# Five seams of a two-layer mLSTM and attention trunk: values ahead of the recurrence, later gate steps, output-projection weights and banks in other places, squares in groups

## The chip, the cores and the metric

The kernel runs on one core of one Trainium2 chip. The metric is the device time of one execution in microseconds (us); the time quoted for a kernel is the median of its runs. PE is the matmul engine (TensorE), DVE is VectorE, ACT is ScalarE, POOL is GpSimd, SP is the engine that issues most transfers. Arithmetic is float32; inputs and output lie in HBM.

## What is computed

The reference is a trunk of two layers on 1024 positions of width 1024. Cut to what matters here:

```python
def hybrid_layer(x, norm1_g, w_in, conv_w, gate_i_b, gate_f_b, head_norm_g, w_out, norm2_g, w_up, w_down):
    h = rms_norm(x, norm1_g)
    mq, mk, mv, mo, mi, mf, aq, ak, av = jnp.split(h @ w_in, ..., axis=-1)
    mq, mk = split(silu(centred_depthwise_conv(concat([mq, mk]), conv_w)))     # 5 taps
    gi = mi + gate_i_b;  gf = log_sigmoid(mf + gate_f_b)                       # per head and direction
    hm = mlstm_chunkwise(q, k, v, gi[0], gf[0]) + flip(mlstm_chunkwise(flip(q), ...))   # 4 heads of 128
    y_m = rms_norm_per_head(hm) * head_norm_g * sigmoid(mo)
    y_a = dilated_attention(rope(aq), rope(ak), av)                            # 8 heads of 64
    x = x + concat([y_m, y_a]) @ w_out
    u = relu(rms_norm(x, norm2_g) @ w_up)                                      # 1024 -> 4096
    return x + (u * u) @ w_down                                                # 4096 -> 1024

def reference(x, ...):
    for layer in range(2): x = hybrid_layer(x, ...)
    return rms_norm(x, final_g)
```

## The kernel before, in words

The activations lie transposed: 128 features on the partitions, 1024 positions along them, in two halves (tiles t = 0 and 1) of 512. Every float32 product is made of three matmuls on values split in a high and a low part: `wh`·high, `wh`·low, `wl`·high. A weight tile is fetched by SP, cast to `wh` by ACT (L80) and its remainder `wl` is made by POOL (L82). A matmul of 512 columns is the unit of most of the work.

A layer runs in this order. `norm` (L141) splits the scaled input in `hh` (ACT, L158) and `hl` (DVE, L159) and sums the squares of the eight feature tiles: `sumsq` makes a square on ACT (L106) and adds it to `acc` (L107, POOL for t = 0 and DVE for t = 1 in layer 1); there each tile's squares stand right behind its split. `gates` (L186 to 278) is a generator that computes the gate rows in three steps, each started by a `next(gates)`: the first up to the norm's `r` and the gates' projection (into PSUM tile `ps`), the second the scans on DVE and a small matmul `pa` (L253) on a row `X` (L250), the third the transposes of the gate rows to `nat` (L276, L277).

Then four mLSTM heads. `m_proj` (L281) makes four projections of a head, each 48 matmuls into two `pj` tiles (three `pj` banks in all): values (`zv`), queries and keys (`z`, then `c` by a 5-tap convolution, one ACT step L301 and four DVE steps L303), output gate (`so`). `evac_r` (L170) brings a `pj` tile to SBUF by a DVE multiply with `r` (L173). `q` and `k` are multiplied with their sigmoid at L325 (keys on DVE, queries on POOL). `m_head` (L331) builds the decay matrices `E` (a transfer, POOL L340, DVE L341), transposes `k` (PE L357), makes the chunk scores (PE L363) and runs the recurrence of eight chunks in two directions (PE L379, L381, L390; DVE L395). `m_tail` (L400) of the head before divides and sums the two directions (DVE L406 to L410, POOL L410 for the second direction, DVE L413), normalises, and transposes the result. The instructions that fill PE during a recurrence are those of the next head's projections.

Eight attention heads follow in four pairs; `a_vt` (L551) transposes a pair's values on PE (L560) and ACT copies them out (L562). During the last pair the first two of seven products of the output projection run (`out_early`, L892).

The output, up and down projections use `seven` (L820): seven products in place of eight on 2x2 blocks. `fetch` (L780) brings weight blocks `w0`, `w1`, `w2` by SP; `plus` (L787) adds another block onto one by an accumulating transfer issued by POOL (L788); `operand`, `diff` and `negsum` (L764 to L778) make the split activations (ACT cast L760, DVE L761, L770, L776). `products` (L799) issues the matmuls (L812) of one product, and `take` adds the finished banks onto the result (`add`, L818). `bank` (L790) hands out the four `ph` banks, which several products share, or in turn three `pj` and one `pi`. In the first chunk of the up projection the norm's sums of `acc` over the partitions are made on PE (`rms`, L129).

Within an engine the order of the instructions is the order of the program unless a scheduler lets a ready instruction pass: `high_priority` (L172) moves an evacuation ahead of its place, `in_order` (L724) keeps the attention as written. The pools' `order` lists (L678, L706, L734) set at which addresses tiles lie and thereby which earlier tiles must be finished before a fetch may start.

## Time and profile before

| | us |
|---|---|
| median of three runs | 2625.42 (2621.58 to 2628.07) |
| the profiled execution | 2632.46 |
| its span | 2630.7 |

| engine | busy us | share |
|---|---|---|
| PE (matmul) | 2466.7 | 94% |
| DVE | 1923.8 | 73% |
| POOL | 1405.3 | 53% |
| ACT | 1252.6 | 48% |

A busy PE is not a PE at its peak: matmuls are pipelined, so the recorded 0.39 us of one overlap those of the next, and where the clock is granted at half, the same matmul takes longer and still counts as busy. How much PE loses at a place is seen in the idle time that a view prints in brackets before an instruction, and in the granted clock of the stretch behind it.

### The profile page before, as it was taken

To read this page: it belongs to the slowest core of one execution; us is meant where nothing else is said; L and a number is where in the kernel's file an instruction comes from. 1 tells how busy PE (TensorE), PEld (TensorE's weight loads), DVE (VectorE), ACT (ScalarE), POOL (GpSimd) and SP (SyncE) were. 2 spreads that over 40 slices of the span, in tenths; PEclk is the share of its full clock that TensorE was granted. 3 is DMA by queue.
4 is the path that set the end of the run, shared out by engine and by line. 5 is a ranking of instruction groups with operands and counts; after the bars stand their busy time and mean duration, and the time that the engine had idled before them with its cause. 6 is when DMAs were issued, how large, how long until landed. Compare 5 with 4: busy or idle time off the path is not lost. (4 is left out here: it accounts for less than half of the span.)

```text
span 2630.7 us, 35982 instructions
## 1 busy us (share of the span) xinstructions
PE 2466.7 (94%) x13470; PEld 1957.5 (74%) x13470; DVE 1923.8 (73%) x2376; ACT 1252.6 (48%) x2092; POOL 1405.3 (53%) x1119
## 2 busy tenths in 40 slices
PE   7899989998999999999898999999989999999997
PEld 5778866666778888787777787666667787887876
DVE  6677666687886786867766776666788767769687
ACT  5444344464654545445444444445455445454544
POOL 4344332335677677767644343223166766767765
PEclk9999999998999999999999999999999999999999
DMA  4222100036455555555322221001365555545553
GB/s 137 89 66 69 42 25 21 27 107 152 95 111 119 102 104 111 104 112 109 90 90 78 69 66 37 25 21 58 108 128 100 105 111 105 112 104 109 113 101 84
DMA packets 119791, 231.39 MB, mean 88 GB/s; under 512 B 14768, under 2 KB 17984, under 8 KB 119616
## 3 DMA queue, kind: packets, MB, share of 16 engines
q0 software_dynamic: 46912, 93.06, 21.3%
q1 hardware_dynamic: 72704, 136.02, 16.5%
q8 instruction: 107, 1.75, 0.3%
q14 instruction: 68, 0.56, 0.1%
HBM read 220.24 MB, written 8.65 MB: 87 GB/s over the span
## 5 line engine op out<-in xcount | busy, mean ns | idle before, releaser
L82 POOL TENSOR_TENSOR wl<-w,wh 128x512 fp32r<-128x512 f32 x484 | 782.7, 1636 | 303.8 <-ACT wh L80 303.3
L812 PE MATMUL ph<-b,wh 128*128 128x512 f32 x2240 | 697.6, 393 | 15.4 <-ACT wh L80 9.8
L812 PEld LDWEIGHTS ph<-b,wh 128*128 128x128 f32 x2240 | 424.3, 190 | 106.0 <-ACT wh L80 11.7
L80 ACT CAST wh<-w 128x512 fp32r<-128x512 f32 x484 | 298.0, 618 | 428.6 <-POOL wl L82 122.7
L812 PE MATMUL ph<-b,wl 128*128 128x512 f32 x1120 | 442.5, 395 | 8.5 <-POOL wl L82 8.0
L82 POOL TENSOR_TENSOR wl<-wr,wh 128x512 fp32r<-128x512 f32 x132 | 200.2, 1519 | 451.0 <-ACT wh L80 432.7
L812 PE MATMUL pj<-b,wh 128*128 128x512 f32 x1224 | 384.0, 395 | 8.0 <-ACT wh L80 8.0
L90 PE MATMUL pj<-hh,wh 128*128 128x512 f32 x896 | 366.9, 410 | 6.4 <-DVE z L173 5.4
L92 PE MATMUL pj<-hh,wl 128*128 128x512 f32 x896 | 358.1, 400 | 0.4 <-POOL wl L82 0.4
L91 PE MATMUL pj<-hl,wh 128*128 128x512 f32 x896 | 356.4, 398 | 0.0
L761 DVE TENSOR_TENSOR b<-T,b 128x1024 fp32r<-128x1024 f32 x148 | 249.6, 1691 | 124.9 <-ACT b L760 119.7
L812 PEld LDWEIGHTS pj<-b,wh 128*128 128x128 f32 x1224 | 233.2, 191 | 59.4 <-ACT wh L80 9.3
L812 PEld LDWEIGHTS ph<-b,wl 128*128 128x128 f32 x1120 | 212.0, 189 | 64.1 <-POOL wl L82 20.6
L812 PE MATMUL pj<-b,wl 128*128 128x512 f32 x612 | 242.3, 396 | 13.5 <-POOL wl L82 13.5
L90 PEld LDWEIGHTS pj<-hh,wh 128*128 128x128 f32 x896 | 171.0, 191 | 54.7 <-issue 15.2
L92 PEld LDWEIGHTS pj<-hh,wl 128*128 128x128 f32 x896 | 170.5, 190 | 35.6 <-POOL wl L82 0.8
L91 PEld LDWEIGHTS pj<-hl,wh 128*128 128x128 f32 x896 | 171.1, 191 | 30.8 <-issue 0.5
L760 ACT CAST b<-T 128x1024 fp32r<-128x1024 f32 x148 | 155.5, 1050 | 44.5 <-DVE T L776 14.6
L788 POOL DMA_DIRECT2D w<-w_down x128 | 116.8, 945 | 74.2 <-DMA w<-w_down 38.3
L601 ACT ACTIVATE sm<-sm,nm 128x512 f32<-128x512 f32 x128 | 91.6, 717 | 131.9 <-DVE nm L599 131.9
L812 PEld LDWEIGHTS pj<-b,wl 128*128 128x128 f32 x612 | 116.6, 191 | 42.3 <-POOL wl L82 18.1
L80 ACT CAST wh<-wr 128x512 fp32r<-128x512 f32 x132 | 80.6, 614 | 139.4 <-PE pj L91 75.6
(254 smaller groups left out, 4268.0 us busy)
## 6 DMA issues: line engine op xcount, KB each, us to landing
w<-w_up SPq DMA_DIRECT2D x128, 256.0 KB, 2.7
w<-w_up POOLq DMA_DIRECT2D x128, 256.0 KB, 4.1
w<-w_down SPq DMA_DIRECT2D x128, 256.0 KB, 2.7
w<-w_down POOLq DMA_DIRECT2D x128, 256.0 KB, 4.2
wr<-w_in SPq DMA_DIRECT2D x116, 256.0 KB, 2.7
E<-gd SPq DMA_DIRECT2D x16, 512.0 KB, 4.8
qi<-gd SPq DMA_DIRECT2D x16, 512.0 KB, 5.6
w<-w_out SPq DMA_DIRECT2D x32, 256.0 KB, 5.3
```

The lines of the kernel that those rows point to most:

```text
L80: nc.scalar.copy(wh, raw)
L82: nc.gpsimd.tensor_tensor(out=wl, in0=raw, in1=wh.bitcast(F32), op=ALU.subtract)
L90: nc.tensor.matmul(ps, wh[:, j, :], xh[:, sl], start=start, stop=False)
L91: nc.tensor.matmul(ps, wh[:, j, :], xl[:, sl], start=False, stop=False)
L92: nc.tensor.matmul(ps, wl[:, j, :], xh[:, sl], start=False, stop=stop)
L601: nc.scalar.activation(sm, sm, AF.Exp, scale=-1.0, bias=nm, accum_out=l)
L760: nc.scalar.copy(hi, src)
L761: nc.vector.tensor_tensor(out=lo, in0=src, in1=hi.bitcast(F32), op=ALU.subtract)
L788: self.nc.gpsimd.dma_start(w, src, accum_op=ALU.add)
L812: nc.tensor.matmul(out, a[:, k, :], b, start=new and k + i == 0, stop=k + i == 5, skip_group_check=not new)
```

## The change

Five places are edited. (1) `m_values`, the values' projection of a head, is taken out of `m_proj` and written ahead of the `m_head` of the head before; head 0's stands ahead of the loop. (2) The second step of the gates comes behind the whole key projection (`i == 1`) and the third behind the output-gate projection. (3) In the output projection `w2` is fetched first and all eight additions onto it are issued at once, then `w1` and `w0`; the `up` pool places `sq` and `w2` ahead of `w1` and `T`; the `dn` pool places the four `ph` banks ahead of `pi`. (4) In layer 1's `norm` the squares stand in groups of four behind the splits of those four tiles. (5) The norm of the first up-projection chunk comes with the second product in place of the first, and `a_vt` copies its groups by DVE and ACT in turn.

```diff
-        for d in order:
+        for i, d in enumerate(order):
 ...
-            if L > 0:
-                squares(d)
+            if L > 0 and i % 4 == 3:
+                for x in order[i - 3:i + 1]:
+                    squares(x)
 ...
-    def m_proj(self, L, h, hs, r, mp, gates):
-
-        nc = self.nc
-        base = 1 + 4 * h
-        ps, self.ahead = self.ahead or self.proj(L, base + 3, hs), None
+    def m_values(self, L, h, hs, r, mp):
+
+        nc = self.nc
+        ps, self.ahead = self.ahead or self.proj(L, 4 + 4 * h, hs), None
         zv = mp.tile([P, S + 4], F32, name="zv", tag="z", bufs=3)
         for t in range(2):
             self.evac_r(zv[:, t * HALF:(t + 1) * HALF], ps[t], r, t)
         v1 = mp.tile([P, NC, P + 1], F32, name="v1", tag=f"v1{h % 2}", bufs=1)
         nc.gpsimd.memset(v1[:, :, P:P + 1], 1.0)
+        return zv, v1
+
+    def m_proj(self, L, h, hs, r, mp, gates, values):
+
+        nc = self.nc
+        base = 1 + 4 * h
+        zv, v1 = values
 ...
-            next(gates, None)
-            if i == 0:
+            if i == 1:
+                next(gates, None)
+            else:
 ...
             self.evac_r(so[:, t * HALF:(t + 1) * HALF], ps[t], r, t)
+        next(gates, None)
 ...
-        for lo, n, m in ((0, 4, 1), (4, 4, 1), (8, 1, 0), (9, 4, 1), (13, 4, 0)):
+        for g, (lo, n, m) in enumerate(((0, 4, 1), (4, 4, 1), (8, 1, 0), (9, 4, 1), (13, 4, 0))):
 ...
-            nc.scalar.copy(dst[:, j:j + n], pt[:, :n])
+            (nc.vector.tensor_copy if g % 2 == 0 else nc.scalar.copy)(dst[:, j:j + n], pt[:, :n])
 ...
-                pend = None
+                pend, values = None, self.m_values(L, 0, hs, r, mp)
                 for h in range(MH):
-                    prj = self.m_proj(L, h, hs, r, mp, gates)
+                    prj = self.m_proj(L, h, hs, r, mp, gates, values)
+                    if h < MH - 1:
+                        values = self.m_values(L, h + 1, hs, r, mp)
 ...
-            self.order(self.up, (("T3", S, 2), ("w1", HALF, 4), ("T", S, 2), ("w2", HALF, 4), ("w0", HALF, 4),
-                                 ("sq", HALF, SQ)))
+            self.order(self.up, (("T3", S, 2), ("sq", HALF, SQ), ("w2", HALF, 4), ("w1", HALF, 4), ("T", S, 2),
+                                 ("w0", HALF, 4)))
             with tc.tile_pool(name=f"dn{L}", bufs=1, space=PSUM, reuse_waits="tile") as self.dn:
+                self.order(self.dn, (("ph", HALF, 4), ("pi", HALF, 1)))
 ...
-        if not early:
-            w0 = self.fetch("w0", src, 0, 0)
-        w1 = self.fetch("w1", src, 0, 1)
-        w2 = self.fetch("w2", src, 1, 0)
         addto = lambda w, m, h: lambda q: self.plus(w[q], src(q, m, h))
         if early:
-            chain = P5 = None
+            w2 = self.fetch("w2", src, 1, 0)
+            for q in range(4):
+                addto(w2, 1, 1)(q)
+            for q in range(4):
+                addto(w2, 0, 0)(q)
+            w1 = self.fetch("w1", src, 0, 1)
             w0 = self.fetch("w0", src, 0, 0)
             for q in range(4):
-                addto(w2, 1, 1)(q)
-                addto(w2, 0, 0)(q)
-            for q in range(4):
                 addto(w0, 1, 0)(q)
+            chain = P5 = None
         else:
+            w0 = self.fetch("w0", src, 0, 0)
+            w1 = self.fetch("w1", src, 0, 1)
+            w2 = self.fetch("w2", src, 1, 0)
 ...
-            if n == 1 and c == 0:
+            if n == 2 and c == 0:
                 self.r2 = self.rms(acc)
```

**What moves on the engines.** The first place is PE in layer 0, head 0, where the transposes of `k` stand. Before, they follow the last matmuls of the output-gate projection (`pj_599`), with the next head's values (`pj_845`) behind them:

```order
L91 MATMUL pj_599<-hl_168,wh_632 128x512
L92 MATMUL pj_599<-hh_167,wl_634 128x512
L357 MATMUL pt_691<-ident_122,c_586 128x128 x4
L357 MATMUL pt_697<-ident_122,c_586 128x128 x4
L90 MATMUL pj_845<-hh_137,wh_849 128x512
L91 MATMUL pj_845<-hl_138,wh_849 128x512
```

After, they (now L366) follow the last matmuls of the next head's values (`pj_671`), with that head's queries (`pj_912`) and the scores (L372) behind them:

```order
L91 MATMUL pj_671<-hl_168,wh_704 128x512
L92 MATMUL pj_671<-hh_167,wl_706 128x512
L366 MATMUL pt_758<-ident_122,c_537 128x128 x4
L366 MATMUL pt_764<-ident_122,c_537 128x128 x4
L90 MATMUL pj_912<-hh_137,wh_916 128x512
L372 MATMUL pt_770<-c_452,c_537 128x128 x4
L372 MATMUL pt_777<-c_452,c_537 128x128 x4
L388 MATMUL pn_786<-v1_383,E_737 128x129
```

All 48 matmuls of the next head's values moved from behind the transposes to in front of them, and the recurrence (L388) is now filled by the next head's queries.

The second place is DVE behind the recurrence of head 0, where the queries of head 1 (`pj_912`, `pj_913`) are brought from their banks (L173, now L174). Before, the values (`zv_907`) had come out during the recurrence, and the queries stand here:

```order
L341 TENSOR_TENSOR E_1143<-nat_379,E_1143 128x1024
L413 TENSOR_TENSOR H_717<-H_717,H_718 128x8x128
L348 COPY dec_1150<-qi_1148 128x8
L417 TENSOR_REDUCE v0_1202<-H_718 128x8
L341 TENSOR_TENSOR E_1152<-nat_379,E_1152 128x1024
L173 TENSOR_TENSOR z_974<-pj_912,r_319 128x512
```

After, in the same place:

```order
L350 TENSOR_TENSOR E_1210<-nat_379,E_1210 128x1024
L357 COPY dec_1217<-qi_1215 128x8
L422 TENSOR_TENSOR H_784<-H_784,H_785 128x8x128
L174 TENSOR_TENSOR z_974<-pj_912,r_319 128x512
L350 TENSOR_TENSOR E_1219<-nat_379,E_1219 128x1024
L174 TENSOR_TENSOR z_974<-pj_913,r_319 128x512
```

The queries' evacuation moved ahead of the second `E` and stays behind the sum `H`; on PE the queries now run a projection earlier, against the recurrence.

The third place is the start of the output projection in layer 0, first on POOL. Before, the remainders of three `w1` weights stand ahead of any addition onto `w2` (the L788 transfers):

```order
L82 TENSOR_TENSOR wl_5642<-w1_5603,wh_5640 128x512
L82 TENSOR_TENSOR wl_5659<-w1_5604,wh_5657 128x512
L82 TENSOR_TENSOR wl_5676<-w1_5605,wh_5674 128x512
L788 DMA w2_5611<-w_out 128x512
L788 DMA w2_5612<-w_out 128x512
```

After:

```order
L800 DMA w2_5608<-w_out 128x512
L800 DMA w2_5605<-w_out 128x512
L82 TENSOR_TENSOR wl_5644<-w1_5621,wh_5642 128x512
L800 DMA w2_5606<-w_out 128x512
L82 TENSOR_TENSOR wl_5661<-w1_5622,wh_5659 128x512
L82 TENSOR_TENSOR wl_5678<-w1_5623,wh_5676 128x512
L800 DMA w2_5607<-w_out 128x512
L800 DMA w2_5608<-w_out 128x512
L800 DMA w0_5629<-w_out 128x512
L800 DMA w0_5630<-w_out 128x512
L82 TENSOR_TENSOR wl_5695<-w1_5624,wh_5693 128x512
```

Five additions moved ahead of the first remainder of `w1`, and four stand between its third and its fourth.

On ACT at the same place the row ahead of the first `w1` weight is, after:

```order
L772 CAST b_5719<-T_5601 128x1024
L772 CAST b_5723<-T_5602 128x1024
L80 CAST wh_5642<-w1_5621 128x512
L80 CAST wh_5659<-w1_5622 128x512
L80 CAST wh_5676<-w1_5623 128x512
L772 CAST b_5756<-T_5601 128x1024
```

Before, one of these casts of a difference `T` stands behind the first three weights:

```order
L80 CAST wh_5640<-w1_5603 128x512
L80 CAST wh_5657<-w1_5604 128x512
L80 CAST wh_5674<-w1_5605 128x512
L760 CAST b_5721<-T_5600 128x1024
L80 CAST wh_5691<-w1_5606 128x512
L760 CAST b_5754<-T_5599 128x1024
```

The second cast of `T` moved ahead of the first weight.

## Rows read from the trace of the kernel before

**Rows 1.** The page's first part: busy us, share of the span, instructions.
```profile
PE 2466.7 (94%) x13470; PEld 1957.5 (74%) x13470; DVE 1923.8 (73%) x2376; ACT 1252.6 (48%) x2092; POOL 1405.3 (53%) x1119
```

**Rows 2.** The chain of work that ended last: start us, us, engine, tile, line.
```profile
2001.09 2.72 PE pi L812 x12
```

**Rows 3.** PE's waits: what for, us in total, times, longest us.
```profile
PE pt L357 <- DVE c L325: 17.5, 4, 7.6
...
PE pa L253 <- DVE X L250: 11.9, 2, 6.6
PE pt L560 <- ACT v L562: 11.7, 8, 2.9
PE ph L812 <- ACT wh L80: 9.8, 3, 5.2
PE pj L812 <- ACT wh L80: 8.0, 2, 4.0
...
PE pn L379 <- DVE E L365: 7.7, 6, 1.3
PE ps L90 <- ACT sq L106: 7.5, 1, 7.5
...
PE ph L812 <- DVE x L818: 5.6, 2, 3.6
PE pj L90 <- DVE z L173: 5.4, 4, 1.7
PE pj L129 <- DVE acc L107: 5.1, 3, 2.1
```

**Rows 4.** Stretches behind waits: PE, PEld, DVE, ACT, POOL busy; PEclk; DMA share; GB/s.
```profile
88.50:93.00 4.50, 4.20 (x14) 3.75 (x15) 4.50 (x7) 1.42 (x2) 1.28 (x1) 0.50 0.17 58
...
626.20:632.20 6.00, 5.86 (x13) 4.16 (x14) 5.01 (x5) 6.00 (x10) 6.00 (x8) 0.50 1.00 161
```

**Rows 5.** Timeline of DVE, layer 0, head 0: start us, us, instruction, [idle before].
```profile
64.01 0.22 DVE L250 TENSOR_SCALAR X<-chunk,X 128x8 f32<-128x8 f32 x1
...
85.88 2.77 DVE L325 TENSOR_TENSOR c<-c,sg 128x1024 f32<-128x1024 f32 x1
```

**Rows 6.** Timeline of PE, head 0: the transposes of k.
```profile
88.80 1.94 PE L357 MATMUL pt<-ident,c 128*128 128x128 f32 x8 [6.43 <-DVE c L325]
```

**Rows 7.** Timeline of DVE behind the recurrences of heads 0 and 1.
```profile
123.42 3.42 DVE L413 TENSOR_TENSOR H<-H 128x1024 f32<-128x1024 f32 x1 [1.80 <-POOL H L410]
...
184.44 1.23 DVE L413 TENSOR_TENSOR H<-H 128x1024 f32<-128x1024 f32 x1
185.58 0.69 DVE L173 TENSOR_TENSOR zv<-pj,r 128x512 f32<-128x512 f32 x1
```

**Rows 8.** Timeline of POOL there; the first row of each head awaits the recurrence's end.
```profile
114.53 0.11 POOL L290 MEMSET v<- 128x8 f32 x1 [15.23 <-PE pn L379]
...
123.36 2.40 POOL L340 TENSOR_TENSOR E<-E,cm 128x1024 f32<-128x1024 f32 x1
...
174.88 0.11 POOL L290 MEMSET v<- 128x8 f32 x1 [17.38 <-PE pn L379]
...
185.13 2.81 POOL L340 TENSOR_TENSOR E<-E,cm 128x1024 f32<-128x1024 f32 x1 [0.59 <-DMA E<-gd]
```

**Rows 9.** Timeline of ACT at the start of layer 0's output projection.
```profile
605.26 1.05 ACT L760 CAST b<-T 128x1024 fp32r<-128x1024 f32 x1 [0.65 <-DVE T L770]
...
607.78 1.04 ACT L760 CAST b<-T 128x1024 fp32r<-128x1024 f32 x1
...
625.39 0.62 ACT L80 CAST wh<-w 128x512 fp32r<-128x512 f32 x1 [5.34 <-DMA w<-w_out]
```

**Rows 10.** Timeline of POOL there.
```profile
606.91 6.13 POOL L82 TENSOR_TENSOR wl<-w,wh 128x512 fp32r<-128x512 f32 x3 [18.34 <-ACT wh L80]
612.99 3.56 POOL L788 DMA_DIRECT2D w<-w_out  x4
```

**Rows 11.** Timeline of DVE, layer 1: the last part of x before the gates.
```profile
1314.01 0.68 DVE L818 TENSOR_TENSOR x<-x,pi 128x512 f32<-128x512 f32 x1
```

## Prediction

> **What bounds the kernel now.** The page's first part comes first: PE is busy for 94% of the span, the next engine for 73% [rows 1]. The chain of waits, followed back from the end, shows the rate: twelve 512-column matmuls in 2.72 us, 0.227 us each [rows 2]. The change adds and removes no matmul, so it can only move time in which PE stands still or runs slowly. Second, PE's own waits, by what they wait for [rows 3]; these are the budget. Third, the granted clock behind long waits: 0.50 of full speed, the lower level of 1.2 GHz [rows 4]. The 6.00 us from 626.2 do the work of 3.0, the 4.50 from 88.5 that of some 2.3. A long wait therefore costs itself and 2 to 3 us more; where no row shows the stretch I take 2.
>
> **Part 1, values ahead and gate steps later.** (a) The wait for X at `pa` is 11.9 us over both layers [rows 3]. `pa` now stands behind the whole key projection, 18 matmuls or 18 x 0.227 = 4.1 us later on PE, while DVE's row that makes X, ending at 64.2 [rows 5], keeps its place behind four conv steps. So 11.9 - 8.2 = 3.7 stay; 8.2 go, and I take half of two slow stretches with them: 2. (b) The wait of the k transposes for c is 17.5 in four places [rows 3]. In head 0 the multiply started at 85.88 and took 2.77 [rows 5], and the transposes started at 88.80 after 6.43 idle [rows 6]. Now 48 matmuls, 10.9 us, stand in front of them; the longest wait was 7.6, so all 17.5 go, with two slow stretches of 2.2: 21.9. (c) The scores now follow the transposes at once and the recurrence's first matmul waits for DVE, as it did six times at up to 1.3 [rows 3]; two more cost 2.6. (d) PE's waits for z, 5.4 in four places [rows 3], came from the old place of the evacuations and go. Gross: 8.2 + 2 + 21.9 - 2.6 + 5.4 = 35.
>
> The price. The recurrence is now filled with the next head's queries. Behind its end (t0) PE has 28 of their matmuls left (6.4 us), eight transposes (1.94 at the lower clock [rows 6], so 0.9) and twelve key matmuls (2.7); then the keys' second tile needs a `pj` bank, the one in which the queries' first tile lies. Its deadline is thus t0 + 10.0. DVE has this evacuation behind the sum of the two directions, L413. In head 1 t0 is 174.9 [rows 8], L413 ends at 185.7 and an evacuation takes 0.69 [rows 7]: t0 + 11.5, a stall of 1.5. In head 0 t0 is 114.5; L413 took 3.42 in place of 1.23, POOL's E having started 0.06 ahead of it [rows 7, 8], and the evacuation would end at t0 + 13.0: a stall of 3.0 and a slow stretch of 2. I take the mean, 3.25, for each of six heads (three in a layer have a next one): 19.5. A second wait is possible where the output gate's second tile needs the keys' bank, whose evacuation stands behind the queries' four conv steps; no row shows it in this order. It lies between 0 and 2 us (a gain is excluded, as there was no wait there to lose), and I take 1: 6. Net 35 - 25.5 = 9.5; bounds: 35 (no price) and 35 - 6 x (5 + 2) = -7.
>
> The page "GPSIMD Engine Reference" of the Trainium skill (section Specifications) says that POOL's SBUF interfaces are shared with DVE, contending with DVE instructions that have two SBUF inputs or run in a two-port mode. The trace agrees with both sides of it: L413, two SBUF inputs, was stretched to 3.42, while the evacuation at 185.58, one of its inputs from PSUM, took 0.69 beside POOL's E of 185.13 [rows 7, 8]. By that rule only what queues ahead of the evacuation is at risk; were the evacuation stretched alike by 2.2, six heads would pay 13 more.
>
> **Part 2, output projection.** Before, PE waits in each layer for ACT's wh, 4.0 and 4.0; then for a wh that waited 5.34 on ACT for its weight's transfer [rows 9], 5.2 and at most 4.6 on PE; then for x, 2.0 and 3.6 [rows 3]. Together 9.8 + 8.0 + 5.6 = 23.4, and six slow stretches, one of 3.0 [rows 4] and five taken as 2: 36.4 in all. The second wait comes from the additions onto w2: POOL stood idle for 18.34 us and then made three remainders ahead of the first of them [rows 10]. Now w2 lies where tiles are free earlier, and five additions stand in that idle stretch. I expect this wait to go, and the one for x behind it, since ACT no longer stands behind a transfer with the casts that DVE needs. In return ACT has one more cast ahead of the first wh: 1.04 and the wait for its difference on DVE, +2.3 (the first cast started at 605.26, the next at 607.78 [rows 9]); and the fourth remainder of w1 stands behind four more issues on POOL at 3.56 / 4 = 0.9 [rows 10], a new wait of 0 to 3, taken as 2. After, per layer: 4.0 + 2.3 + 2 + a slow stretch of 3 = 11.3, twice 22.6. A gain of 14. SP's fetch of w2 comes only as early as the freed addresses allow, which no row shows: if the second and third wait stay, most comes back. Bounds 30 (the first wait does not grow, no new one) and -5.
>
> **Part 3, start of layer 1.** PE waits once for 7.5 us, put down to ACT's square [rows 3]; but the last to come was x from bank pi, which left DVE only at 1314.69 [rows 11]: the gates' bank is pi's bank. With ph's banks, and the squares in groups, the wait for the bank goes; but DVE and POOL have the same additions, now four in a row, beside the high and low parts of the next four tiles, and these must come all the same. Of 7.5 + 2 I take 4; bounds 0 and 9.
>
> **Part 4, norm and copies.** The sums of `acc` waited 5.1 in three places, 2.1 the longest [rows 3]. They come one product, 48 matmuls or 10.9 us, later, and nothing needs r2 before the first finished block; two waits of 2.1 with a slow stretch of 2 each go, less up to 1 for a bank: 7; bounds 2 and 8. The values' transposes wait for ACT's copies, 11.7 in eight places, 2.9 the longest [rows 3]. In the first pair of a layer DVE has a backlog of its own splits, so I let 2 x 2.9 stay; of the other 6 half goes: 3; bounds -3 and 8, since the copies now stand in front of DVE's softmax steps.
>
> **The sum.** 9.5 + 14 + 4 + 7 + 3 = 37.5. The profiled execution took 2632.5, so 2595 for it; it lies 7.1 above the median of the runs, which becomes 2625.4 - 37.5 = 2588.
>
> **Rivals.** A: the seams close nearly wholly. For it: each cover is longer than the wait it covers (10.9 against 7.6; 18.34 of idle POOL against five issues of 0.9). Against: the deadline of t0 + 10.0, which both heads read miss. Part 1 gives 30, part 2 27, the rest 19: 76, time 2549. B: the waits only move. The queries' evacuation comes as in head 0 everywhere and the output gate waits its 2 (part 1: -7); the first wait of the output projection and the new one eat most of the second's (part 2: 5); the rest gives 10: 8, time 2617. For it: DVE and POOL run side by side in just these stretches. Against: head 1's row. C, on the other side: DVE's queue behind the recurrence makes the kernel slower. The place is the evacuation of the queries, the price its delay behind t0 + 10.0 with a slow stretch of 3. Parts 2 to 4 give 28, part 1 gross 35; it decides from (28 + 35) / 6 = 10.5 a head, an evacuation that ends at t0 + 17.5. The two heads read give t0 + 11.5 and 13.0, so it takes two more stretches of 2.2 like that of L413 in every head; at t0 + 19.5 it is 9.5 + 3 = 12.5, six times 75, less 63: 12 slower, 2637. D: the change does not do what it says, and the time stays. The order shows each move, so what is left of D is an equal new wait, which B prices.
>
> **How the numbers follow.** My forecast has 0.5, A 0.22, B 0.22, C 0.06. The predicted time is 2588. The range goes from A's 2549 to just short of B's 2617, 2615; outside lie C, near half of B and a little of A, together about 0.2. A difference of 0.3%, 7.9 us, is about what a measurement of this kernel can tell from no change: faster by more than that are the forecast, A and half of B, 0.84; within it the other half of B, 0.1; slower 0.06.
>
> **What would show it.** In the profile after, the k transposes' wait for c should be gone in head 0 of both layers, and `pa` wait 1 to 3 us. PE should wait for z in up to six places, 1 to 3 us each: none speaks for A, over 7 each for C. At the output projection the first wait for wh should be 6 to 7 us, the second (for a weight in flight) gone; two waits as long as before speak for B. The wait at the start of layer 1 should halve. The forecast is wrong if the granted clock behind the recurrences falls to half in all six heads, or if the values' evacuation, now ahead of the recurrence on DVE, delays its start.

## The result and the profile after

The changed kernel takes 2612.85 us, the median of six runs (2608.03 to 2617.41), beside 2626.81 for the kernel before in the same comparison: a ratio of 0.9943, with a 95% interval of 0.9926 to 0.9961, or 15 us less. The forecast was 37.5 us less. The profiled execution took 2613.13, its span 2611.4; that is 19.3 under the one before, so the two executions compared below differ by 5 us more than the medians do.

The page's first part after: busy us, share of the span, instructions. PE's work is the same; its busy time and the span fell.

```profile
PE 2459.4 (94%) x13470; PEld 1956.7 (75%) x13470; DVE 1919.9 (74%) x2400; ACT 1237.2 (47%) x2064; POOL 1396.7 (53%) x1119
```

PE's waits after, as in [rows 3]: what for, us in total, times, longest. L824 is the product of the output projection and the MLP (L812 before), L90 a projection's matmul, L366 and L372 the transposes of k and the scores' first matmuls, L569 the transposes of the attention's values.

```profile
PE pj L824 <- POOL wl L82: 22.6, 9, 6.2
PE pj L90 <- DVE z L174: 18.5, 8, 2.6
...
PE pj L824 <- ACT wh L80: 12.6, 2, 6.3
...
PE pt L372 <- ACT kn L367: 6.8, 2, 4.9
PE pt L569 <- DVE v L571: 6.3, 2, 3.2
...
PE pt L569 <- ACT v L571: 3.6, 8, 0.7
PE pa L254 <- DVE X L251: 3.3, 1, 3.3
PE pj L824 <- DVE u L830: 2.9, 2, 1.5
PE pt L366 <- DVE c L334: 2.8, 2, 1.7
PE pn L388 <- DVE E L374: 2.6, 2, 1.3
PE pt L569 <- DVE l L611: 2.2, 2, 1.1
...
PE pj L129 <- DVE u L830: 1.8, 2, 0.9
...
PE pj L129 <- DVE acc L107: 1.0, 1, 1.0
```

Most waits that the change aimed at are shorter. Those for the copies of the values are not: 6.3 for DVE's, 3.6 for ACT's and a new 2.2 for `l` stand where 11.7 stood before [rows 3]. Four waits that were shorter or absent are now long: z from 5.4 to 18.5, the remainder `wl` up to 6.2 in one place of each layer, the first cast `wh` from 4.0 to 6.3, and `kn`, which is new. Where the 19.3 us lie follows from the start times of matching PE instructions in both executions:

| stretch | after less before, us | forecast, us |
|---|---|---|
| recurrent part, layer 0 and layer 1 | -0.8, -4.4 | -9.5 for both |
| output projection, layer 0 and layer 1 | -3.7, -3.7 | -14 for both |
| start of layer 1 | -2.4 | -4 |
| norm behind the output projection, both layers | -1.1, -0.7 | -7 for both |
| attention, both layers (the copies) | -0.2, +1.3 | -3 for both |
| rest of the MLP, layer 0 and layer 1 | -0.1, -3.4 | 0 |

For the last row the prediction has no term. In the traces of the changed kernel and of all fourteen kernels below, also of those that take back the banks, the places or the norm, the rest of the MLP is 0.1 to 5.2 us shorter in layer 0 and 1.3 to 7.7 in layer 1 than in the one trace of the kernel before. That speaks for an execution before that was long there, and not for a gain of the change, but neither is shown.

Two places of the changed kernel show what happened. **The output projection of layer 0**, PE first: start us, us, instruction, [idle before].

```profile
608.08 1.22 PE L824 MATMUL pj<-b,wh 128*128 128x512 f32 x2 [6.29 <-ACT wh L80]
615.49 0.79 PE L824 MATMUL pj<-b,wl 128*128 128x512 f32 x1 [6.19 <-POOL wl L82]
```

POOL there, and below it DVE in the same us:

```profile
608.11 7.33 POOL L82 TENSOR_TENSOR wl<-w,wh 128x512 fp32r<-128x512 f32 x1 [7.25 <-ACT wh L80]
```

```profile
607.42 1.22 DVE L782 TENSOR_TENSOR T<-y 128x1024 f32<-128x1024 f32 x1
608.55 1.22 DVE L773 TENSOR_TENSOR b<-T,b 128x1024 fp32r<-128x1024 f32 x1
609.69 2.36 DVE L788 SCALAR_TENSOR_TENSOR T<-y,T 128x1024 f32<-128x1024 f32 x2
611.96 1.22 DVE L782 TENSOR_TENSOR T<-y 128x1024 f32<-128x1024 f32 x1
613.10 1.22 DVE L773 TENSOR_TENSOR b<-T,b 128x1024 fp32r<-128x1024 f32 x1
```

And the stretch as a whole, columns as in [rows 4]:

```profile
607.00:620.60 13.60, 6.33 (x14) 4.55 (x15) 7.75 (x8) 3.94 (x7) 12.49 (x8) 0.50 0.29 66
```

Three remainders took 6.13 together before [rows 10]; here the first alone took 7.33, and its end, 615.44, is 1.1 behind the end of DVE's last row, 614.32. DVE's six two-input instructions (the third row holds two; the first was running when POOL began) took 1.2 us each. PE made one pair of matmuls, stood for 6.19, and the whole stretch ran at a granted clock of 0.50, the lower level. Layer 1 shows the same: 7.33 again, a wait of 6.2.

**Head 0 of layer 0**, at the end of the recurrence. DVE's queue, then the matmul that waits for it:

```profile
120.72 3.39 DVE L422 TENSOR_TENSOR H<-H 128x1024 f32<-128x1024 f32 x1
124.03 0.68 DVE L174 TENSOR_TENSOR z<-pj,r 128x512 f32<-128x512 f32 x1
...
136.00 1.28 DVE L174 TENSOR_TENSOR z<-pj,r 128x512 f32<-128x512 f32 x2
```

```profile
124.77 0.50 PE L90 MATMUL pj<-hh,wh 128*128 128x512 f32 x1 [2.45 <-DVE z L174]
```

This is the stall the prediction priced: the queries' evacuation behind the stretched sum of the two directions. It stands in all six heads, 2.36 to 2.62 us each. The keys' evacuation comes late too, at 136.00 behind four conv steps of q; here PE does not wait for it, but in two other heads a second wait (2.16 and 1.50) follows.

### The profile page after: what moved, and what is told of

Its sections match the earlier page's. It is cut to its first block, busy times and chain, and to the rows that moved or that the text cites. A ratio compares the mean times of both kernels' runs of the same rounds, so it can differ in the third digit from the quotient of the medians.

```text
span 2611.4 us, 35967 instructions
## 1 busy us (share of the span) xinstructions
PE 2459.4 (94%) x13470; PEld 1956.7 (75%) x13470; DVE 1919.9 (74%) x2400; ACT 1237.2 (47%) x2064; POOL 1396.7 (53%) x1119
## 5 line engine op out<-in xcount | busy, mean ns | idle before, releaser
L824 PE MATMUL ph<-b,wh 128*128 128x512 f32 x2240 | 690.3, 389 | 0.0
L824 PEld LDWEIGHTS ph<-b,wh 128*128 128x128 f32 x2240 | 420.3, 188 | 87.4 <-ACT wh L80 0.6
L824 PE MATMUL ph<-b,wl 128*128 128x512 f32 x1120 | 438.4, 391 | 7.5 <-POOL wl L82 7.3
L82 POOL TENSOR_TENSOR wl<-wr,wh 128x512 fp32r<-128x512 f32 x132 | 187.8, 1424 | 405.3 <-ACT wh L80 384.2
L824 PE MATMUL pj<-b,wh 128*128 128x512 f32 x1224 | 383.0, 395 | 17.2 <-ACT wh L80 12.6
L90 PE MATMUL pj<-hh,wh 128*128 128x512 f32 x896 | 369.0, 412 | 19.6 <-DVE z L174 18.5
L773 DVE TENSOR_TENSOR b<-T,b 128x1024 fp32r<-128x1024 f32 x148 | 242.4, 1641 | 127.9 <-ACT b L772 122.8
L824 PEld LDWEIGHTS pj<-b,wh 128*128 128x128 f32 x1224 | 232.7, 191 | 68.8 <-ACT wh L80 13.9
L824 PE MATMUL pj<-b,wl 128*128 128x512 f32 x612 | 241.9, 395 | 22.6 <-POOL wl L82 22.6
L824 PEld LDWEIGHTS ph<-b,wl 128*128 128x128 f32 x1120 | 210.2, 188 | 59.6 <-POOL wl L82 16.5
L90 PEld LDWEIGHTS pj<-hh,wh 128*128 128x128 f32 x896 | 171.5, 191 | 69.6 <-DVE z L174 21.9
L824 PEld LDWEIGHTS pj<-b,wl 128*128 128x128 f32 x612 | 116.4, 190 | 51.4 <-POOL wl L82 27.2
```

What stands on the lines that cost most here:

```text
L82: nc.gpsimd.tensor_tensor(out=wl, in0=raw, in1=wh.bitcast(F32), op=ALU.subtract)
L90: nc.tensor.matmul(ps, wh[:, j, :], xh[:, sl], start=start, stop=False)
L773: nc.vector.tensor_tensor(out=lo, in0=src, in1=hi.bitcast(F32), op=ALU.subtract)
L824: nc.tensor.matmul(out, a[:, k, :], b, start=new and k + i == 0, stop=k + i == 5, skip_group_check=not new)
```

## The experiments

Each kernel is the changed kernel with the edit named, timed beside the kernel before on its chip (medians of 2625.68 to 2629.82 there), so ratios are what is compared; the changed kernel's is 0.9943. Differences in us between kernels are those of the medians unless said otherwise; by the ratios they come out up to 3 us otherwise.

### The output projection: is the seam worth anything, and what ate it?

**The seam undone.** The order and the places of w0, w1 and w2, and the additions, as before:

```diff
-            self.order(self.up, (("T3", S, 2), ("sq", HALF, SQ), ("w2", HALF, 4), ("w1", HALF, 4), ("T", S, 2),
-                                 ("w0", HALF, 4)))
+            self.order(self.up, (("T3", S, 2), ("w1", HALF, 4), ("T", S, 2), ("w2", HALF, 4), ("w0", HALF, 4),
+                                 ("sq", HALF, SQ)))
...
+            w0 = self.fetch("w0", src, 0, 0)
             for q in range(4):
                 addto(w2, 1, 1)(q)
-            for q in range(4):
                 addto(w2, 0, 0)(q)
```

> The changed kernel with the output projection's part taken back: the up pool's addresses, the order of fetches and the order of the additions are those of before; the banks and all other seams stay changed. From the last attention matmul to the first matmul of the up projection the changed kernel is 3.65 us (layer 0) and 3.72 us (layer 1) shorter than the one before. Theory S (the new places did remove the waits for the weight in flight and for x, but most of it was given back by the first remainder, which POOL finished only after 7.33 us): this stretch is 3 to 5 us longer again in each layer, the waits are 4.0, 0.5 to 1, 4.3 to 5.4 and 2 to 3.8 as before, no wait of 6 us for a remainder; the time 6 to 10 us above the changed kernel. Rival M (the gain of that stretch comes from elsewhere, the banks or the clock): the stretch stays within 1.5 us of the changed kernel's.

Measured: 2620.91, 0.9978 [0.9962, 0.9994], 8 us over the changed kernel. Up to the first matmul of the up projection, the stretch is 3.5 us longer than in the changed kernel in layer 1, but only 0.7 in layer 0, where rival M's bound of 1.5 would hold. There, however, PE waits 2.04 for a remainder in the up projection's first product, and with that product counted in both stretches are longer by 3.1 and 3.5, within 0.6 of the kernel before. Its waits for `wh` are back, and those for x in part (1.0 and 1.8, where 2.0 and 3.6 stood):

```profile
PE ph L824 <- ACT wh L80: 8.4, 2, 5.0
PE pj L824 <- ACT wh L80: 8.0, 2, 4.0
```

So the seam is worth some 7 us, half of the 14 forecast. The wait of 6.2 for the remainder comes with it: here the longest at that place is 1.0.

**The remainders of w1 on DVE** in place of POOL, in the output projection only:

```diff
-            nc.gpsimd.tensor_tensor(out=wl, in0=raw, in1=wh.bitcast(F32), op=ALU.subtract)
+            (eng or nc.gpsimd).tensor_tensor(out=wl, in0=raw, in1=wh.bitcast(F32), op=ALU.subtract)
...
-        ps = self.products(w1, op)
+        ps = self.products(w1, op, eng=self.nc.vector if early else None)
```

> The changed kernel, but the four remainders of the output projection's first product are made by DVE in place of POOL. Theory S (POOL's first remainder is shut out while DVE runs five instructions with two SBUF inputs in a row): PE's wait of 6.2 us for the first remainder falls under 1.5 us in both layers, the slow stretch of 13.6 us behind it shortens by half or more, and the output projection's stretch shortens by 5 to 9 us per layer; time 10 to 16 us under the changed kernel. Rival D (the remainder is late because DVE has too much to do there, whoever makes it): the wait stays at 3 us or more, or moves to the casts of the next product, and the stretch shortens by under 2 us.

Measured: 2598.98, 0.989 [0.9862, 0.9918], 14 us under the changed kernel. The waits of 6.2 are gone; the stretch is 7.7 and 7.5 us shorter than before in the two layers, against 3.7 and 3.7 in the changed kernel, a gain of 4 in each, under the 5 to 9 expected. DVE takes 0.69 for what POOL took 7.33 for, between its own instructions:

```profile
604.85 1.22 DVE L782 TENSOR_TENSOR T<-y 128x1024 f32<-128x1024 f32 x1
605.98 0.69 DVE L82 TENSOR_TENSOR wl<-w,wh 128x512 fp32r<-128x512 f32 x1
606.59 1.23 DVE L773 TENSOR_TENSOR b<-T,b 128x1024 fp32r<-128x1024 f32 x1
```

The two stretches together are now 15.2 under the kernel before, which is what the seam was to bring (14). Of the 14 us against the changed kernel only 7.8 lie in them. In the traces the rest lies in the MLP, which this edit leaves alone and in which kernels differ by several us; the intervals of the two ratios leave anything from 5 to 23 for the whole.

**The first cast in two halves**, so that POOL's remainder begins at another moment of DVE's instruction. This parts two forms of the reason: POOL is held until DVE's run of such instructions ends, or it misses one moment by chance.

```diff
-            nc.scalar.copy(wh, raw)
+            for a, b in ((0, 2), (2, 4)) if cut else ((0, 4),):
+                nc.scalar.copy(wh[:, a:b], raw[:, a:b])
```

> The changed kernel, but ACT casts the first w1 weight of the output projection in two halves, so that POOL's first remainder starts some 0.2 us later against DVE's instructions; nothing else differs. Theory S1 (shut out by a missed moment: POOL's start fell 0.445 us ahead of DVE's next instruction, where in the kernel before, at 0.457, POOL got in between and DVE waited): PE's wait for the first remainder falls from 6.2 us to 1 to 2 in both layers and DVE's next instruction is stretched to 2.3; time 6 to 12 us under the changed kernel. Rival S2 (any remainder that meets such a run of DVE instructions is held to its end): the wait is 6.0 us again, the time the same.

Measured: 2615.69, 0.9951 [0.9937, 0.9965]. The remainder ran from 606.56 to 612.61, again to the end of DVE's run, and PE waited 5.28:

```profile
612.66 0.80 PE L825 MATMUL pj<-b,wl 128*128 128x512 f32 x1 [5.28 <-POOL wl L83]
```

POOL began 0.30 us ahead of DVE's next instruction in place of 0.44, and this other moment did not free it: in both kernels it was held until the run ended.

**The casts of T later.** ACT makes them only behind the first three `wh`, so the first `wh` comes without the 2.3 us that the prediction counted.

```diff
-        op = self.diff(T, B11, B12)
+        if early:
+            with self.tc.issue_after(self.wh2.ins):
+                op = self.diff(T, B11, B12)
+        else:
+            op = self.diff(T, B11, B12)
```

> The changed kernel, but on ACT the two casts of the next product's difference T stand behind the first three w1 weights of the output projection, not ahead of them; DVE's two remainders of T, which need these casts, so stand behind its four differences. Theory K (the casts ahead of the first weight are what lengthens PE's first wait from 4.0 to 6.3 us): this wait returns to 4.0 to 4.3 in both layers. On the second wait, 6.2 us for POOL's first remainder: if POOL is held until DVE's run of two-input instructions ends, it shortens with the run, DVE having four differences of 1.22 in place of the five instructions it had, of which two or three lie behind POOL's start, to 2 to 4 us; if POOL gets in between, to under 1.5. Time 4 to 16 us under the changed kernel. Rival (the first weight itself is late): both waits as before, time the same.

Measured: 2613.07, 0.9948 [0.9932, 0.9965], the time of the changed kernel, where 4 to 16 us less were expected. The first wait fell from 6.29 to 2.33, below the 4.0 expected, and the one for the remainder from 6.19 to 1.57. POOL, starting 3 us earlier beside the same run of DVE, was not held, and this time DVE paid: its five instructions took 11.6 us.

```profile
604.96 2.22 POOL L82 TENSOR_TENSOR wl<-w,wh 128x512 fp32r<-128x512 f32 x1 [3.92 <-ACT wh L80]
```

```profile
605.97 6.74 DVE L782 TENSOR_TENSOR T<-y 128x1024 f32<-128x1024 f32 x3
612.63 4.89 DVE L773 TENSOR_TENSOR b<-T,b 128x1024 fp32r<-128x1024 f32 x2
```

x then came late (a wait of 4.1 on PE at `ph` in layer 0, of 2.5 in layer 1), and the stretches came out at -2.8 and -4.05 against the kernel before: as in the changed kernel. One engine was held or the other, and the gain at the first wait was given back at the next.

### The waits for z: one place in DVE's queue, or two?

**The queries' evacuation ahead of the sum** of the two directions. The theory (Z) was that the stall behind each recurrence goes with it.

```diff
-        nc.vector.tensor_tensor(out=hsum, in0=hsum, in1=H[1][:, :, 0:P], op=ALU.add)
+        with self.tc.issue_after(self.qev.ins):
+            nc.vector.tensor_tensor(out=hsum, in0=hsum, in1=H[1][:, :, 0:P], op=ALU.add)
```

> The changed kernel, but on DVE the sum of the two directions is issued behind the evacuation of the next head's first query tile, which so moves one place ahead; nothing else differs. Theory Z (that place is what makes PE wait for z, 18.5 us in eight places, with four slow stretches of 3.4 us behind): of the first wait of each head, 2.5 to 2.8 us, at most 1 stays; the waits for z fall to 6 or less in total, and the mLSTM part of both layers together is 12 to 22 us shorter; time 10 to 20 us under the changed kernel. Rival Z2 (the evacuation is late because of what stands ahead of the sum as well, the division and E stretched by POOL): each wait falls by less than 1.2 us, the part by under 8 us.

Measured: 2611.32, 0.9932 [0.991, 0.9953]: not to be told from the changed kernel. The evacuation did come earlier, at 121.22 in place of 124.03, and the first wait went in all six heads. But the keys' evacuation did not move (136.61 against 136.00), and PE stood there:

```profile
121.22 0.68 DVE L174 TENSOR_TENSOR z<-pj,r 128x512 f32<-128x512 f32 x1
121.82 2.90 DVE L425 TENSOR_TENSOR H<-H 128x1024 f32<-128x1024 f32 x1
...
136.61 1.28 DVE L174 TENSOR_TENSOR z<-pj,r 128x512 f32<-128x512 f32 x2
```

```profile
137.35 0.80 PE L90 MATMUL pj<-hh,wh 128*128 128x512 f32 x1 [3.34 <-DVE z L174]
```

Six waits of 3.3 to 3.9 took the place of eight of 1.5 to 2.6. Theory Z fell: DVE's queue had two late evacuations in a row.

**Both evacuations ahead.** As above, and the last three conv steps of q behind the keys' first evacuation in heads 1 to 3 (theory Q); the values' transposes now stand ahead of all conv steps in the code:

```diff
-                nc.vector.scalar_tensor_tensor(out=c, in0=z[:, j:j + S], scalar=cw[:, j:j + 1], in1=c,
-                                               op0=ALU.mult, op1=ALU.add)
+                if h > 0 and i == 0 and j >= 2:
+                    with self.tc.issue_after(kev.ins):
+                        step()
+                else:
+                    step()
```

> As the experiment z_early, and besides the last three of the queries' four convolution steps on DVE stand behind the evacuation of the first key tile (heads 1 to 3), so that both evacuations that PE waits for come as soon as DVE is at them. z_early moved the first wait of 2.6 us to the second place and left the sum. Theory Q (what is late there is DVE's queue as a whole, and the two evacuations need only be put ahead of work that nobody waits for yet): PE's waits for z fall from 18.5 (changed kernel) and 21.3 (z_early) to under 8 us, and the mLSTM part of both layers together shortens by 10 to 20 us. Rival W (DVE and POOL together are the bound behind each recurrence; the convolution is now late for the key transposes): the waits for z fall but the k transposes wait for c or the scores for kn by as much, and the part shortens by under 5 us.

Measured: 2590.64, 0.9863 [0.9841, 0.9885], 22 us under the changed kernel. The waits for z are 0.6 in all; the keys' evacuation comes at 128.08. The wait for c grew from 2.8 to 8.4. The longest waits left in the recurrent part:

```profile
PE pt L378 <- DVE c L346: 8.4, 2, 4.6
...
PE pt L384 <- ACT kn L379: 6.8, 2, 6.0
```

The attention of layer 0 begins at 313.5, against 328.2 before and 327.4 in the changed kernel (below). The recurrent part of both layers is 22 us shorter than in the changed kernel, where theory Q expected 10 to 20. The price of part 1 was thus real, 22 us where the prediction counted 25.5, and it hangs on two places in one queue. The edit also moves the values' transposes and the conv steps; what part they have in the 22 was not tried.

### Values and gate steps: which of the two moved c?

**The gate steps later, the values back.** The theory (V) was that the wait for c returns, since the cover that the prediction counted, 48 matmuls, is taken away.

```diff
-                pend, values = None, self.m_values(L, 0, hs, r, mp)
+                pend = None
                 for h in range(MH):
-                    prj = self.m_proj(L, h, hs, r, mp, gates, values)
-                    if h < MH - 1:
-                        values = self.m_values(L, h + 1, hs, r, mp)
+                    prj = self.m_proj(L, h, hs, r, mp, gates, self.m_values(L, h, hs, r, mp))
```

> The changed kernel with the values' projection back at its old place, inside its own head; the gates' later steps and all other seams stay changed. The mLSTM part of the changed kernel is 0.8 (layer 0) and 4.4 us (layer 1) shorter than that of the kernel before, where I had forecast 5 a layer. Theory V (the new place removes the k transposes' wait for c, 17.5 us with its slow stretches, but pays it back in waits for z, 13 us more, and for kn, 6.8): the waits for c return, 12 to 18 us, those for z fall to 5 or 6 and those for kn to under 1; the part lies within 6 us of the changed kernel's in each layer. Rival G (the new place is a clear gain and the later gate steps are what costs): the part is 8 us or more longer than the changed kernel's in each layer.

Measured: 2597.62, 0.9889 [0.9866, 0.9912]: 15 us under the changed kernel, and the wait for c does not return. Theory V fell, and so did rival G: the recurrent part is 13 us shorter than in the changed kernel, not longer.

```profile
PE pn L388 <- DVE E L374: 15.1, 8, 3.8
...
PE pt L366 <- DVE c L334: 4.6, 3, 2.2
```

PE waits 3.6 for X at `pa` and 2.6 for z in all. The wait for E at `pn` is the price: 15.1, where 7.7 stood before [rows 3]. DVE's timeline tells why c is early. Here the multiply of c stands ahead of the first step of E, for which DVE waits on POOL:

```profile
77.82 1.22 DVE L334 TENSOR_TENSOR c<-c,sg 128x1024 f32<-128x1024 f32 x1
...
84.92 3.35 DVE L350 TENSOR_TENSOR E<-nat,E 128x1024 f32<-128x1024 f32 x1 [4.03 <-POOL E L349]
```

In the kernel before, this row of E stands in front of the multiply, which follows at 85.88 [rows 5] behind one evacuation:

```profile
82.01 3.35 DVE L341 TENSOR_TENSOR E<-nat,E 128x1024 f32<-128x1024 f32 x1 [3.55 <-POOL E L340]
```

The sigmoid that c is multiplied with was ready at 79.78 there and is ready at 77.51 here, so of the 8.1 us between 85.88 and 77.82 the order on DVE accounts for 5.8.

**The values ahead, the gate steps in their old places.** The rival (N) was that the two parts matter only together, or little.

```diff
-            if i == 1:
-                next(gates, None)
-            else:
+            next(gates, None)
+            if i == 0:
...
-        next(gates, None)
         last = None
```

> The changed kernel with the gates' steps back at their old places, the values' projection still ahead of the recurrence: the fourth corner beside before (neither), the changed kernel (both) and the experiment no_values (gate steps alone, 15 us under the changed kernel). Theory G (the later gate steps are the gain of the mLSTM part, some 7 us in layer 0 and 14 in layer 1; the values' new place is a loss of 6 and 10 through waits for z): the wait for X at the gates' small matmul is 5 to 7 us again in both layers, the waits for z stay near 18, and the time is 2620 to 2632, that is 8 to 18 us above the changed kernel. Rival N (the two parts lean on each other: with the values ahead there is cover enough whatever the gates do): within 5 us of the changed kernel.

Measured: 2614.84, 0.9956 [0.9939, 0.9974], 2 us over the changed kernel, as rival N has it; theory G had put it 8 to 18 over.

```profile
PE pj L90 <- DVE z L174: 20.5, 9, 2.6
...
PE pa L254 <- DVE X L251: 12.0, 2, 6.6
...
PE pt L364 <- DVE c L332: 2.2, 2, 1.1
```

The cover alone does hide c (2.2), at 20.5 of z; X waits 12.0 again.

**Both undone**, all other seams kept: whether c's wait and DVE's old order come back together, and what the two are worth as a pair (theory O in the text).

> The changed kernel with both parts of the mLSTM seam taken back, values and gate steps; the other seams stay changed. It is the fourth corner: gate steps alone came out 15 us under the changed kernel, values alone 2 us above it. Theory O (the k transposes' wait for c comes from DVE's order: in the kernel before the multiply that makes c is queued behind head 0's first E, for which DVE stood idle 3.55 us; the later gate steps put it ahead of E, as in no_values, where it starts at 77.8 in place of 85.9; the values' new place only covers the same wait and costs waits for z): the waits for c are 16 to 18 us again, those for X 11 to 12, and the time is 2615 to 2625, 3 to 12 us above the changed kernel and 18 to 25 above the gate steps alone. Rival (the gain of the gate steps alone came from X's wait only): under 10 us between this kernel and the gate steps alone.

Measured: 2609.87, 0.9923 [0.9906, 0.994]. c waits 15.1 in four places, and DVE has the order of the kernel before again: E first, behind 3.54 of idling, c after it.

```profile
83.07 1.22 DVE L348 TENSOR_TENSOR E<-nat,E 128x1024 f32<-128x1024 f32 x1 [3.54 <-POOL E L347]
...
84.81 2.78 DVE L332 TENSOR_TENSOR c<-c,sg 128x1024 f32<-128x1024 f32 x1
```

The order is as theory O says, but its time is not: 3 to 12 us over the changed kernel were expected and it is 3 under; 18 to 25 over the gate steps alone, and it is 12, or 9 by the ratios. The rival, that X's wait alone makes the gain of the gate steps, had put the latter under 10. The waits decide against the rival: from this kernel to the gate steps alone PE's waits for X fall from 12.0 to 3.6, those for c from 15.1 to 4.6 and those for z from 5.3 to 2.6, while those for E at `pn` rise from 7.7 to 15.1. Together that is 14.2 less, and the recurrent part is 15.1 shorter.

The four corners, with the recurrent part of both layers read from the start times (start of the program to the attention of layer 0, and the norm's sums of layer 1 to its attention; 626.3 in the kernel before). Kernels with that part unchanged differ by up to 4 us in it.

| | gate steps at old places | gate steps later |
|---|---|---|
| values in their old place | 0.9923, 623.0 | 0.9889, 607.9 |
| values ahead | 0.9956, 627.9 | 0.9943, 621.0 |

The row of the transposes that open the attention gives the end of layer 0's part: 327.4 in the changed kernel, 321.5 with the gate steps alone, 313.5 with both evacuations ahead. Columns: tile, count, ns, first and last start us.

```profile
L569 PE MATMUL pt<-ident,vt x136: 270/283/489, 327.4 to 1840.4; 128*128 128x128 f32 x136
```

```profile
L569 PE MATMUL pt<-ident,vt x136: 270/283/489, 321.5 to 1823.8; 128*128 128x128 f32 x136
```

```profile
L582 PE MATMUL pt<-ident,vt x136: 270/283/422, 313.5 to 1815.2; 128*128 128x128 f32 x136
```

So the gate steps alone gain 15 us of the part (9 by the whole time); the values' move alone gains nothing (5 worse, near what such parts vary by); and beside the later steps it gives back 13. As a pair they are worth 2 us of the part, and by the whole time they cost 5: neither can be told from nothing, since the intervals around 0.9943 and 0.9923 overlap. With the evacuations mended, the pair reaches 599.0, better than the steps alone.

**Head 0's product of q on DVE.** The new wait for `kn` comes behind a chain from POOL's E over DVE's E and ACT's exponential to the copy; the theory (E) was that POOL's product of q (2.76 us) ahead of E is what delays it, the rival (T) that the transfer of E from HBM does.

```diff
-        for c, eng in zip(qk[::-1], (nc.vector, nc.gpsimd)):
+        for c, eng in zip(qk[::-1], (nc.vector, nc.vector if h == 0 else nc.gpsimd)):
```

> The changed kernel, but in head 0 of each layer the queries' multiply with their sigmoid is made by DVE in place of POOL, so that POOL reaches the two decay matrices E of head 0 2.8 us earlier. In the changed kernel the scores of head 0 wait for kn, 2.2 and 5.2 us; ACT has that copy behind the exponential of the second E, which waits for DVE and POOL. Theory E (the chain POOL, DVE, ACT of E sets the start of head 0's recurrence, now that the k transposes are covered): the waits for kn fall by 2 us or more each and head 0's recurrence ends 2 to 4 us earlier in both layers. Rival T (E's transfer from HBM, which comes later since the gates' steps are later, sets it): no change over 1 us.

Measured: 2612.03, 0.9941 [0.9925, 0.9957]; PE still waits 6.4 for `kn`. Theory E fell, and the trace shows what T says: with q's product gone from its queue POOL began E at 82.56, no earlier than in the changed kernel (82.18), since it had to wait for the transfer, 0.30 us here and 1.64 in layer 1.

```profile
82.56 5.90 POOL L349 TENSOR_TENSOR E<-E,cm 128x1024 f32<-128x1024 f32 x2 [0.30 <-DMA E<-gd]
```

In the changed kernel ACT's order shows besides that the exponentials, which wait for DVE's E, stand ahead of the copies:

```profile
91.58 1.06 ACT L352 ACTIVATE E<-E 128x1024 f32<-128x1024 f32 x1 [4.15 <-DVE E L350]
...
93.05 1.06 ACT L367 COPY kn<-pt 128x512 f32<-128x512 f32 x2
```

Another order on ACT was not tried by itself. With the gate steps alone the copies do stand ahead (83.64); there the recurrence's first matmul waits 3.68 for E instead, so that the wait may only change its name.

### The small seams

**Squares, norm and copies as before**, the banks kept:

```diff
-            if L > 0 and i % 4 == 3:
-                for x in order[i - 3:i + 1]:
-                    squares(x)
+            if L > 0:
+                squares(d)
...
-            (nc.vector.tensor_copy if g % 2 == 0 else nc.scalar.copy)(dst[:, j:j + n], pt[:, :n])
+            nc.scalar.copy(dst[:, j:j + n], pt[:, :n])
...
-            if n == 2 and c == 0:
+            if n == 1 and c == 0:
```

> The changed kernel with three seams in three separate stretches taken back: layer 1's squares behind each tile, the norm of the up projection behind its first product, and all copies of the transposed values on ACT; the banks stay changed. By the two profiles the changed kernel is 2.4 us shorter than before from the last matmul of layer 0's down projection to the norm's sums in layer 1, 1.2 and 0.8 us shorter around the up projection's norm, 0.2 us shorter and 1.3 us longer in the attention of layers 0 and 1. Theory P (each is what its stretch shows): the start of layer 1 is 1 to 4 us longer than in the changed kernel, the norms 0.5 to 2.5 each, the attention 0 to 1.5 shorter; together 2 to 8 us above the changed kernel. Rival B (the gain at the start of layer 1 is the banks' alone): that stretch does not change, by 0.7 at most.

Measured: 2617.49, 0.9967 [0.9949, 0.9984]. The start of layer 1 is 3.4 us longer than in the changed kernel, the norm's stretches 1.1 and 1.9 longer, the attention 0.7 and 0.2 shorter. The copies thus bring nothing, and in sum the waits they aimed at did not shrink either: PE waits 11.7 for them here, 6.3, 3.6 and 2.2 in the changed kernel.

**The banks as before:**

```diff
-                self.order(self.dn, (("ph", HALF, 4), ("pi", HALF, 1)))
```

> The changed kernel with the banks of the projections placed as before (pi ahead of ph), nothing else. Theory B (in the kernel before, layer 1's gates waited 7.5 us for pi's bank, which is evacuated last): the wait in front of the gates' first matmul returns, 4 to 8 us, and the start of layer 1 is 2 to 7 us longer than in the changed kernel. Rival Q (the squares in groups alone removed that wait): no wait over 2 us there and a change of under 1 us.

Measured: 2609.34, 0.9941 [0.992, 0.9962]: no difference. The wait for the bank is back,

```profile
PE ps L90 <- DVE x L829: 6.2, 1, 6.2
```

but three waits for weights and their remainders that the changed kernel has in the same place (1.85, 1.03 and 1.88) are gone, and the start of layer 1 is only about 1 us longer. The squares in groups carry that seam, not the banks.

### Together

**Both evacuations ahead and w1's remainders on DVE**: whether the two gains add.

> The two fixes together: the evacuations of the first query tile and the first key tile put ahead as in z_both (22 us under the changed kernel), and the remainders of the output projection's first product made by DVE as in wl_dve (14 us under it). If the two causes are separate, as the stretches in which they lie say, the gains add: 34 to 38 us under the changed kernel, 2575 to 2580, a ratio of 0.980 to 0.982 to the kernel before. If they share a cause (the clock, or DVE's and POOL's common port), less than 28.

Measured: 2580.65, 0.9829 [0.9803, 0.9855]: 45 us under the kernel before and 32 under the changed one, faster than both. The two gains alone were 22 and 14, so 32 of 36 are there, a little under the 34 to 38 expected.

**The gate steps alone (values back) and w1's remainders on DVE**: a simpler way, perhaps as good.

> The gate steps later without the values ahead (15 us under the changed kernel), and the remainders of the output projection's first product made by DVE (14 us under it). If the two add, 2583 to 2586, against 2580.65 for the other pair of fixes; if they share the cause, 2590 or more.

Measured: 2591.47, 0.9858 [0.9842, 0.9873]. By the medians only 6 of the 14 us of the remainders are added here, by the ratios 8; a shared cause had been put at 2590 or more. The start times decide: the remainders on DVE make the two output-projection stretches 8.1 us shorter here than with the gate steps alone, 8.2 in the kernel above against both evacuations ahead, and 7.8 against the changed kernel. They are worth 8 us each time, and the rest of the 14 was no part of them. The recurrent part stays as short as with the gate steps alone (606.8 against 607.9).

## Why the prediction was right and wrong

**Direction right, size wrong.** 15 of 37.5 us came. By the start times part 1 brought 5.2 (9.5 forecast), part 2 7.4 (14), part 3 2.4 (4), the norm 1.8 (7), and the copies lost 1.1 (3 gained). The time, 2612.85, lies near rival B's 2617 (the waits only move), in part by luck: B had part 1 at a loss of 7 and the small seams at a gain of 10. B's first ground, POOL and DVE side by side in these stretches, is what the runs found in the output projection; in the recurrent part it was order in DVE's queue.

**Part 1, gross 35: (b) came out, by half of its reason.** It put c's wait down to missing cover and credited all 17.5 us and 4.4 of slow clock to the 48 matmuls. The wait did fall, to 2.8, and with the values ahead alone it falls to 2.2. But before, c was late chiefly because it stood behind a row of DVE that idled 3.55 us for POOL's E. The later gate steps put c ahead of that row, and alone they leave 4.6 of the wait. So two halves of one seam removed the same wait, and the cover paid its price for what the other half gave at a price of 7.4 at `pn`. The prediction had read which instruction ended the wait, and not what that one stood behind.

**In part 1 a term was put at nothing.** With c early, the scores' first matmuls wait for `kn`, 6.8 in two places; (c) put a loss of 2.6 at `pn`, which fell from 7.7 to 2.6 instead, and nothing here. That the two nearly cancel is luck. Since this part differs by up to 4 us between executions, most of the 4.3 missing here may be no more than that. (a) was right: 3.7 forecast for X, 3.3 found. (d) is borne out as far as can be seen: the eight waits for z that are there are those priced below.

**Part 1, the price: right, with its mechanism.** The wait begins 10.0 to 10.2 us behind the recurrence's end in all six heads, where the deadline was t0 + 10.0, and the evacuation ends at t0 + 12.4 to 12.8, between the two readings of 11.5 and 13.0; the sum ahead of it was stretched to 3.4 in each. 3.25 a head with the slow clock was forecast; the stall is 2.36 to 2.62 in each of six heads, and a second wait (bounds 0 to 2) stands in two at 2.16 and 1.50. With both evacuations put ahead 22 us came back, against 25.5 priced. What the page "GPSIMD Engine Reference" of the Trainium skill (section Specifications) says of shared interfaces agrees with the rows here too: the sum of 120.72, two SBUF inputs, took 3.39 beside POOL's E (2.38 us from 120.65), while 28 evacuations of the changed kernel with one input in PSUM lie beside a tensor operation of POOL for nine tenths of their time or more, and none took over 0.70.

**Part 2, 14: the term for the new wait failed.** The wait for a weight in flight went and so did the one for x, and the first wait came out at 6.29 (6.3 forecast). But the new wait, "0 to 3, taken as 2", was put at the fourth remainder, behind queued issues. It came at the first, at 6.19 in both layers. So PE stands still in the two stretches for 25.0 us, as long as before (25.1, of which the prediction took 23.4 from [rows 3]), where 16.6 was forecast. What was gained, 7.4, is slow clock, and that was sized rightly: an estimate by 192 matmuls at the 0.227 us of [rows 2], 43.5 a layer, leaves 14.5 us besides the waits for both stretches before and 7.3 after, a gain of 7.2 where 13 less 6 was forecast. The earlier cast had been the prediction's 2.3; what it moved POOL's remainder into, a run of DVE's two-input instructions, was not looked at. With the remainders on DVE the two stretches gain 15.2.

**Part 3, 4: the right size nearly, by another ground.** 2.4 came, and the run with the old banks bears out that the bank was not the limit. But what is left there is not the additions, as the prediction had it: PE's waits are for a cast and for remainders, 1.85, 1.03 and 1.88.

**Part 4: both terms too large, since the waits moved.** Two of the norm's three waits went (5.1 to 1.0), but waits for u of 0.9 and 1.5 in each layer stand in these stretches, 2.3 where 2.1 stood, and 1.8 of 7 were left. Of the copies' 11.7 some 6.3 stay, now for DVE's copies in the first pair of each layer, as the prediction allowed (2 x 2.9). Of the other 6 half was to go; 3.6 stay and 2.2 for `l` are new, and the attention was no shorter.

## What to carry to other kernels

Before a wait is covered with other work, follow its releaser one step further: if that instruction stands in its own engine's queue behind one that idles, changing the order may be cheaper than a cover: here it made the recurrent part 15 us shorter, and the cover nothing. When work is put ahead of a stage, write down each evacuation that its banks need, in the queue's order; with two late ones in a row, mending the first showed no gain here, and mending both 22 us. An instruction moved to another time must be checked against what the engine that slows it, or that it slows, is doing at the new time. And a gain in the whole time should be looked for in the stretch that was edited: of 14 us that one edit seemed to bring, 8 lay there.

## What the runs showed of the hardware that was not expected

A POOL instruction with two SBUF inputs can be held for several DVE instructions, not for one. In the changed kernel it was held 7.33 us through five of them that began after it, each at 1.2 us; with the cast in halves it took 6.05, and both times it ended 1.1 us behind the last DVE instruction of the run. With the casts later POOL got in (2.22) and DVE was stretched instead, 11.6 us for five that need 1.2 each. The Trainium skill's page "SBUF — State Buffer" (section "SBUF: two separate sides") says that the shared pair of ports is an exclusive lock: of a DVE instruction with two SBUF inputs and a GpSimd instruction that reads SBUF, the one that starts first has it for its whole instruction, and the other blocks. The runs agree that one blocks while the other goes on; they add that the one that waits isn't always the next to be served. Such holds are rare: of the changed kernel's 616 remainders on POOL three took over 4 us, these two and one of 4.65, and of the kernel before none took over 3.51. In [rows 7, 8] it is DVE that waits: POOL's E began 0.06 us ahead of DVE's sum, which was stretched to 3.42. What decides who is held, and for how long, was not found.
